# Hybrid decoder layer on one core: planner prices, slab release times, slack, and the sums of the last norm

## The chip, the cores and the metric

One core of one Trainium2 chip runs the whole layer in one launch. The metric is device time in microseconds (us). The kernel before was timed three times: 1110.89, 1110.3 and 1108.43 us, median 1110.3.

Engines are named as the profile names them: PE (TensorE matmuls), PEld (its weight loads), DVE (VectorE), ACT (ScalarE), POOL (GpSimd) and SP (SyncE, which issues all DMAs here).

## The reference, cut to what matters

One trunk layer on `x` of 1024 tokens by 1024 channels, float32, followed by a final RMSNorm:

```python
h = rmsnorm(x, norm_mix_w); proj = h @ w_in                # 3072 main columns + 8 gate logits
qkv = silu(causal_conv4(qkv)); q, k = l2norm(q), l2norm(k) # 4 heads of 128
o = gated_delta_rule_chunked(q, k, v, g, beta)             # per chunk: (I + A)^-1, then a scan of states
gdn_out = rmsnorm(o, gdn_norm_w) * silu(z)
lru_out = rg_lru(causal_conv4(lru_x) + b, ...) * gelu(lru_gate)   # 512 channels
x = x + concat(gdn_out, lru_out) @ w_out
u = relu(rmsnorm(x, norm_mlp_w) @ w_ff1)
x = x + (u * u) @ w_ff2
return rmsnorm(x, final_norm_w)
```

## The kernel before, in words

Channels lie on the 128 partitions and tokens along the free dimension; the 1024 tokens are two halves (`hf`) of 512. The common tile is a "slab" of 128x512 float32; there are 84 of them (`NS`). Each float32 product is made of three float32r matmuls (high x high, high x low, low x high).

The program has these stages: 24 column tiles of the input projection (matmuls into `pj`), between which the work of the four heads and of the LRU is placed; the output projection (`po`); the first feed-forward product (`pf`) and the second (`p`), both as a seven-product scheme for 2x2 blocks; and the last norm.

No engine's order is written by hand. The layer is first recorded as a list of operations, and `Plan.emit` then simulates the engines: `price` gives each operation a cost, `lag` the time until another engine sees its result, and the next operation is the one that can start first, with due times breaking near ties. The real instructions are issued in that order, so all of them carry line 376, where `emit` calls the engine. At run time each engine works through its own list in order and waits on semaphores where an operand or a buffer isn't ready. What the planner believes decides only the order and which buffer an operation gets.

Places that the change and the prediction touch:

- `price`, line 283: the cost of a POOL operation on n elements of a partition. `emit` adds a lag of 0.1 us between POOL operations that depend on each other.
- `admit`, line 298: a PE operation due between 30 and 1000 is held ready `SLACK` us later after an operand from another engine. The projections' own matmuls are due from 10000 on and have no such slack.
- `room` and lines 357 to 362: an operation that writes a new slab takes one that the plan has free by then, the latest one released. Line 382 notes when a slab is free again: 0.2 us after its last user's planned end.
- `invert32` and `rows32` (lines 768 to 808): POOL inverts the 32x32 diagonal blocks of a head, in 31 rounds of a product into `tm` and a subtraction from `V`. Round m reads the slab `N[m // 16]`. SP then moves the result into `Y`.
- `gd_k`, `gd_u`, `gd_q`, `gd_inv`, `gd_scan`: the heads' PE units between the projection's matmuls; `psK`, `psA`, `psP`, `psZ`, `pvs`, `psO` are their PSUM banks (eight banks in all). `gd_inv` begins with a DVE transpose of `Y` into a slab `YT`. `evac` empties a projection bank into `p` on DVE.
- The end, lines 1465 to 1479: the last product is done in two halves of 256 tokens. For each of four row tiles, `plus` adds the bank to `u2` on DVE, `squares` squares it on ACT, and `normed` sums the squares over partitions with matmuls against `onesd` into `n3p`, one pair of columns for each part; then come the root, `n3b`, and the scaled output `ot`.

Of the kernel before, what the change touches and what calls it, by code (L numbers as in the profile page):

```python
# [32 lines left out]
LOOK = 4  # L33
AHEAD = 100
TAIL = 4
SLACK = 1.3
LAND = 2.0
LATE = 2.5
SMALL = ("bv", "tr")
# [29 lines left out]
def lag(a, b):  # L69
    return LAG[a, b] if (a, b) in LAG else LAG_FROM[a] + (0.12 if b == "pe" else 0.0)  # L70
# [114 lines left out]
class Plan:  # L185
# [77 lines left out]
    @staticmethod  # L263
    def price(e, method, args, kw):
        out = kw.get("out", args[0] if args else None)
        src = [v for k, v in kw.items() if isinstance(v, View) and k in ("in_", "in0", "in1", "data0")]
        shape = out.shape if isinstance(out, View) else src[0].shape
        n = 1
        for d in shape[1:]:
            n *= d  # L270
        if e == "sy":
            return n * shape[0] * 4 / 300e3
        psum = any(v.root.tag == "m" for v in src)
        ptr = sum(isinstance(kw.get(k), View) for k in ("scalar", "scalar1", "scale", "bias"))
        if e == "ve":
            if method == "reciprocal":
                return 0.06 + 0.0066 * n
            return 0.067 + n * (0.00104 if method in TWO or psum else 0.00052) + 0.06 * ptr
        if e == "ac":
            return 0.0008333 * n + (0.051 if psum else 0.094) + 0.093 * ptr + (0.093 if "accum_out" in kw else 0.0)  # L280
        if method == "memset":
            return 0.036 + 0.00083 * n
        return 0.2 + 0.0021 * n

    def emit(self, engines, caps):
        ops = self.ops
# [6 lines left out]
        slots = {t: [(0.0, k) for k in range(n)] for t, n in caps.items()}  # L293
        table, dma = None, 0.0

        def admit(o):
            for e in o.engines:
                late = SLACK if e == "pe" and o.due < 1000.0 and o.due > 30.0 else 0.0
                ready[e].append((max([d.end + lag(d.eng, e) + (late if d.eng != "pe" else 0.0) for d in o.deps], default=0.0), o))

        def loads(o):

            return o.table is not None and o.table != table and not (o.table == "any" and table in WITH_TANH)
# [13 lines left out]
        def choose(strict):  # L317
            pick = None
            for e, lst in ready.items():
                if not lst:  # L320
                    continue
                look = []
                for t, o in (sorted(lst, key=lambda x: (x[1].due, x[1].seq))[:10] if e == "sy" else lst):
                    rt = room(o, strict)
                    if rt is None:
                        continue
                    s = max(t, free[e], rt)
                    if len(o.engines) > 1 and any(max(free[x], t) + o.cost[x] < s + o.cost[e] for x in o.engines if x != e):
                        continue
                    look.append((s, o))  # L330
                if not look:
                    continue
                first = min(s + HOLD * loads(o) for s, o in look)
                best = None
                for s, o in look:
                    if s + HOLD * loads(o) > first + WAIT[e]:
                        continue
                    key = o.due + SWITCH * loads(o)
                    if best is None or (key, o.seq) < best[0]:
                        best = (key, o.seq), s, o  # L340
                if pick is None or best[1] < pick[1]:
                    pick = e, best[1], best[2]
            return pick
# [4 lines left out]
        for _ in range(len(ops)):  # L348
            pick = choose(True) or choose(False)
            if pick is None:  # L350
                left = [o for o in ops if o.eng is None and not o.wait]
                raise RuntimeError("no room: " + ", ".join(f"{o.engines}.{o.calls[0][0]}:{[r.nm for r in o.roots if r.real is None]}" for o in left[:30])
                                   + str({t: len(s) for t, s in slots.items()}))
            e, s, o = pick
            for x in o.engines:
                ready[x] = [q for q in ready[x] if q[1] is not o]
            for r in o.roots:
                if r.real is None:
                    sl = slots[r.tag]
                    r.slot = max((x for x in sl if x[0] <= s), default=min(sl))  # L360
                    sl.remove(r.slot)
                    r.real = r.make(r.slot[1])
            c = o.cost[e]
            if e == "sy":
                small = any(r.tag in SMALL for r in o.roots)
                free[e] = s + (0.62 if small else 0.45)
                dma = max(dma, free[e] + 0.65) + c
                o.end = dma + (LATE if small else LAND)
            else:
                if loads(o):  # L370
                    table = "exp" if o.table == "any" else o.table
                    c += LOAD
                free[e] = o.end = s + c
            o.eng = e
            for method, args, kw in o.calls:
                getattr(engines[e], method)(*[v.ap() if isinstance(v, View) else v for v in args],  # L376
                                            **{k: v.ap() if isinstance(v, View) else v for k, v in kw.items()})
            for r in o.roots:
                r.users -= 1
                r.end = max(r.end, o.end)  # L380
                if not r.users:
                    slots[r.tag].append((r.end + 0.2, r.slot[1]))
            for q in o.next:
                q.wait -= 1
                if not q.wait:
                    admit(q)
# [4 lines left out]
def layer(ctx: ExitStack, tc: tile.TileContext, xT, win, wba, prm, cst, wga, wgx, wout, w1, w2, out):  # L391
# [4 lines left out]
    pe, ve, ac, gp, sy = (pl.engine(n) for n in engines)  # L396
# [9 lines left out]
    def slab(nm, dt=F32):  # L406
        return pl.tile(sp, [P, 512], dt, "s", nm)

    def pair(nm, dt=F32):
        return [slab(nm + "0", dt), slab(nm + "1", dt)]  # L410

    def bank(nm):
        return pl.tile(mpool, [P, 512], F32, "m", nm)
# [31 lines left out]
    def mm3(ps, w, x, first, last, order=((0, 0), (0, 1), (1, 0))):  # L445
        n = 0
        for a, b in order:
            pe.matmul(ps, lhsT=w[a], rhs=x[b], start=first and n == 0, stop=last and n == 2)
            n += 1
# [91 lines left out]
    def when(i):  # L541

        return 14.0 * i
# [448 lines left out]
    def chain(t):  # L992
        return pl.at(due=t)
# [9 lines left out]
    with pl.at(due=-2000.0):  # L1003
        for hf in range(2):
            hs = slice(hf * 512, hf * 512 + 512)
            ps0 = [bank(f"g0_{i}") for i in range(2)]
            ss = slab("ss1")
            for k in range(KT):
                pl.due = -2000.0 + 10 * k + 100 * hf
                if hf == 0:  # L1010
                    xraw[0, k] = slab("xraw")
                    sy.dma_start(out=xraw[0, k], in_=xT[k * P:(k + 1) * P, hs])
                    if k in (0, 2, 4):
                        n = 4 if k == 4 else 2
# [101 lines left out]
    ss = pair("ss2")  # L1116
# [31 lines left out]
    for n, d in enumerate(DO):  # L1148
        i = len(MT) + n
        t = when(i)  # L1150
        split(i + 1)
        for hf in range(2):
# [6 lines left out]
            with chain(t + 7 + 7 * hf):  # L1159
# [3 lines left out]
                x = bm[d, hf] = slab("bm")  # L1163
# [21 lines left out]
    def tf(g):  # L1185
        return t0 + g * 19.1
# [32 lines left out]
    for g in range(NG):  # L1219
        t = tf(g)  # L1220
        ps, y = {}, {}
# [60 lines left out]
    def ts(st, g):  # L1282
        return begin[st] + g * 2.72 * len(STAGES[st])
# [50 lines left out]
    def wsl(g, i, d):  # L1334
        return tuple(t[:, d * P:(d + 1) * P] for t in W2[g, i])
# [7 lines left out]
    def plus(x, y):  # L1343
        ve.tensor_tensor(out=x, in0=y, in1=x, op=ALU.add)
# [40 lines left out]
    def squares(x, n=512):  # L1385
        y = slab("sq3")[:, 0:n]
        ac.activation(out=y, in_=x, func=AF.Square)
        return y
# [6 lines left out]
    for st, prods in enumerate(STAGES):  # L1395
        tail = TAIL if st == 3 else 0
        pd = {}
        for g0 in range(0, NG, 2):
# [6 lines left out]
            for d in range(4):  # L1405
                for i in prods:
# [10 lines left out]
                    with chain(ts(st, g0) - 100):  # L1417
                        if i in (1, 7, 5):
                            x = {1: p1, 7: u3, 5: p5}[i][d] = slab(f"p{i}_")
# [10 lines left out]
            for x, k, g in residual[st]:  # L1430
                if g in gs:
                    with chain(ts(st, g) + 3):
                        plus(x[k[0] % 4], load_x2(*k, st, g))
                        if x is p5:
                            y = squares(p5[k[0] % 4])
                            if k[0] == 4:
                                ss = y
                            else:
                                plus(ss, y)
        t = begin[st] + 87  # L1440
# [7 lines left out]
        if st == 2:  # L1448
            with chain(t - 40):
                s1 = None  # L1450
                for x in [p1[d] for d in range(4)] + [u3[d] for d in range(4)]:
                    y = squares(x)
# [6 lines left out]
    t = ts(3, NG - TAIL)  # L1459
# [5 lines left out]
    for o in (0, 256):  # L1465
        qs = slice(o, o + 256)
        parts = []
        for d in range(4):
            ps = bank("p2")[:, 0:256]
            for g in range(NG - TAIL, NG):  # L1470
                with pl.at(due=10000.0 + t + o / 50 + 0.1 * d), pl.unit(PIECE / 2):
                    mm3(ps, wsl(g, 3, d), tuple(x[:, qs] for x in UU[g, 3]), g == NG - TAIL, g == NG - 1)
            with chain(t - 100):
                x = u2[d][:, qs]
                plus(x, ps)
                parts.append((squares(x, 256), t))
        parts.insert(1, (ss[:, qs], t))
        X = [u2[d][:, qs] for d in range(4)] + [p5[d][:, qs] for d in range(4)]
        normed(X, parts, 512 + o, 256, t + o / 50, [4, 5, 6, 7, 0, 1, 2, 3], True)

# [64 lines left out]
```

## Time and profile before

| | |
|---|---|
| runs | 1108.43 to 1110.89 us, median 1110.3 |
| profiled execution, its own time | 1107.9 us |
| its span, first to last instruction | 1105.8 us |
| mean granted PE clock | 0.993 |
| PE busy | 1087.3 us (98%), 5399 matmuls |
| DVE busy | 864.8 us (78%) |
| ACT busy | 552.1 us (50%) |
| POOL busy | 100.5 us (9%), 282 instructions |

Times of the trace are counted from the span's start. A row of a stretch in order of time has start, duration, engine, line, operation, output and inputs with their shapes, the count where several were merged, and in brackets the idle time of the engine ahead of it with what ended it. Busy PE time includes matmuls that run at a lower clock, and ends of matmuls are modelled. Who ended a wait is inferred from semaphores.

### The profile page before, as it was taken

How to read it: one execution, taken by the hardware profiler on the slowest of the kernel's cores; microseconds unless marked ns; L12 is line 12 of the kernel's file. 1: busy time of each engine (PE TensorE's matmuls, PEld its weight loads, DVE VectorE, ACT ScalarE, POOL GpSimd, SP SyncE). 2: the span in 40 equal slices, each digit the busy share in tenths (PEclk: the TensorE clock that was granted, in tenths of full speed). 3: DMA queues.
4: the chain of work that ended last, by engine and by line, in shares of the span. 5: the costliest groups of instructions: out<-in, count | busy, mean ns of one | idle time of the engine just before them, and what ended most of it. 6: DMA issues, size and time to landing. Idle time of an engine off the chain costs nothing. (4 is left out here: it accounts for less than half of the span.)

```text
span 1105.8 us, 15998 instructions
## 1 busy us (share of the span) xinstructions
PE 1087.3 (98%) x5399; PEld 895.7 (81%) x5399; DVE 864.8 (78%) x1672; ACT 552.1 (50%) x1134; POOL 100.5 (9%) x282
## 2 busy tenths in 40 slices
PE   9999989999999999999999999999999999999996
PEld 7788867888787878888888888888888888888886
DVE  7878665797779776598988888887965767865796
ACT  8559634545485955453333333333444544564442
POOL 0004857026000000000000000000000000000000
PEclk9999989999999999999999999999999999999998
DMA  7133513233212144424544444434856565677382
GB/s 239 39 96 86 125 27 103 68 89 97 78 58 58 39 152 133 153 95 147 197 146 158 146 160 143 171 140 174 283 179 220 180 206 184 206 237 241 125 296 84
DMA packets 124225, 159.17 MB, mean 144 GB/s; under 512 B 56392, under 2 KB 59120, under 8 KB 124144
## 3 DMA queue, kind: packets, MB, share of 16 engines
q1 hardware_dynamic: 124144, 158.16, 44.3%
q8 instruction: 42, 0.69, 0.3%
q14 instruction: 39, 0.32, 0.1%
HBM read 115.11 MB, written 43.01 MB: 143 GB/s over the span
## 5 line engine op out<-in xcount | busy, mean ns | idle before, releaser
L376 PE MATMUL pj<-xh,w 128*128 128x512 f32 x704 | 244.9, 406 | 0.5 <-DVE p L376 0.5
L376 PEld LDWEIGHTS pj<-xh,w 128*128 128x128 f32 x704 | 133.1, 189 | 28.6 <-DVE p L376 1.1
L376 PE MATMUL pj<-xl,w 128*128 128x512 f32 x352 | 138.2, 393 | 0.0
L376 ACT ACTIVATE c<-c 128x512 f32<-128x512 f32 x64 | 40.4, 632 | 85.6 <-DVE c L376 80.7
L376 PE MATMUL po<-mxh,w 128*128 128x512 f32 x256 | 79.3, 390 | 0.8 <-ACT mxh L376 0.8
L376 ACT CAST w<-r 128x512 fp32r<-128x512 f32 (+1 forms) x62 | 51.3, 828 | 54.7 <-PE pf L376 37.8
L376 DVE SCALAR_TENSOR_TENSOR y<-p,pr,y 128x512 f32<-128x512 f32 (+3 forms) x96 | 71.5, 750 | 6.5 <-ACT y L376 4.1
L376 PEld LDWEIGHTS pj<-xl,w 128*128 128x128 f32 x352 | 66.9, 190 | 10.5
L376 DVE TENSOR_TENSOR w<-r,w 128x512 fp32r<-128x512 f32 (+1 forms) x62 | 58.7, 947 | 19.2 <-ACT w L376 18.8
L376 POOL TENSOR_TENSOR tm<-V,N 128x60 f32<-128x60 f32 (+24 forms) x124 | 48.4, 390 | 128.6 <-DMA N<-bn 69.3
L376 PEld LDWEIGHTS po<-mxh,w 128*128 128x128 f32 x256 | 48.0, 188 | 11.1 <-ACT mxh L376 1.2
L376 PE MATMUL po<-mxl,w 128*128 128x512 f32 x128 | 49.9, 390 | 0.7 <-DVE mxl L376 0.7
L376 POOL TENSOR_TENSOR V<-V,tm 128x60 f32<-128x60 f32 (+24 forms) x124 | 45.3, 365 | 9.7
L376 DVE SCALAR_TENSOR_TENSOR c<-c,n2B 128x512 f32<-128x512 f32 x64 | 43.8, 689 | 1.2
L376 PE MATMUL pf<-B5h,w 128*128 128x512 f32 x128 | 42.7, 394 | 0.0
L376 PE MATMUL pf<-B6h,w 128*128 128x512 f32 x128 | 42.3, 390 | 0.0
L376 ACT ACT_TABLE_LOAD x27 | 34.6, 1283 | 3.5 <-DVE y L376 2.4
L376 DVE TENSOR_TENSOR c<-pf,u 128x512 f32<-128x512 f32 x48 | 32.8, 686 | 0.5
L376 ACT CAST v6h<-s 128x512 fp32r<-128x512 f32 x16 | 10.0, 622 | 41.0 <-DVE s L376 41.0
L376 PEld LDWEIGHTS pf<-B5h,w 128*128 128x128 f32 x128 | 24.0, 188 | 6.9 <-DVE c L376 2.0
L376 PE MATMUL p<-u3h,v3h 128*128 128x512 f32 (+1 forms) x80 | 28.4, 355 | 0.7 <-DVE u L376 0.7
L376 PEld LDWEIGHTS po<-mxl,w 128*128 128x128 f32 x128 | 24.0, 188 | 6.0 <-DVE mxl L376 1.0
(512 smaller groups left out, 2976.2 us busy)
## 6 DMA issues: line engine op xcount, KB each, us to landing
w2r<-w SPq DMA_DIRECT2D x112, 256.0 KB, 3.5
ur<-ud SPq DMA_DIRECT2D x112, 256.0 KB, 4.9
r<-w SPq DMA_DIRECT2D x32, 512.0 KB, 3.7
ud<-c SPq DMA_DIRECT2D x64, 256.0 KB, 2.1
ud<-ut SPq DMA_DIRECT2D x48, 256.0 KB, 2.1
r<-win SPq DMA_DIRECT2D x22, 512.0 KB, 4.0
xraw<-xT SPq DMA_DIRECT2D x16, 256.0 KB, 5.2
r<-wout SPq DMA_DIRECT2D x8, 512.0 KB, 4.5
```

Of the source, the lines that this page charges most:

```text
L376: getattr(engines[e], method)(*[v.ap() if isinstance(v, View) else v for v in args], **{k: v.ap() if isinstance(v, View) else v for k, v i ...
```

## The change

A POOL operation is priced at 0.22 + 0.0023 n in place of 0.2 + 0.0021 n. `SLACK` is 1.0 in place of 1.3. A slab or a DRAM tile whose last planned user runs on POOL (`gp`) or is a DMA of SP (`sy`) counts as free 2.0 us after that user's end, where it was 0.2; all others stay at 0.2. In the end stage, the squares of row tiles 0 to 2 and the earlier sum `ss` are added up on DVE into one tile, and `normed` gets two parts (that sum and the squares of tile 3) in place of five.

```diff
-SLACK = 1.3
+SLACK = 1.0
...
-        return 0.2 + 0.0021 * n
+        return 0.22 + 0.0023 * n
...
-                    slots[r.tag].append((r.end + 0.2, r.slot[1]))
+                    slots[r.tag].append((r.end + (2.0 if e in ("gp", "sy") else 0.2), r.slot[1]))
...
                 x = u2[d][:, qs]
                 plus(x, ps)
-                parts.append((squares(x, 256), t))
-        parts.insert(1, (ss[:, qs], t))
+                y = squares(x, 256)
+                if d == 0:
+                    plus(y, ss[:, qs])
+                    parts.append((y, t))
+                elif d < 3:
+                    plus(parts[0][0], y)
+                else:
+                    parts.append((y, t))
         X = [u2[d][:, qs] for d in range(4)] + [p5[d][:, qs] for d in range(4)]
```

## Rows read from the trace of the kernel before

**Rows 1.** The page's first part: busy time, share and instructions of each engine.
```profile
PE 1087.3 (98%) x5399; PEld 895.7 (81%) x5399; DVE 864.8 (78%) x1672; ACT 552.1 (50%) x1134; POOL 100.5 (9%) x282
```

**Rows 2.** PE's waits, 100 to 400 us: us in total, times, longest.
```profile
PE psA L376 <- DVE p L376: 3.8, 1, 3.8
PE po L376 <- ACT mxh L376: 0.8, 1, 0.8
PE psP L376 <- DVE S L376: 0.7, 1, 0.7
PE po L376 <- DVE mxl L376: 0.7, 1, 0.7
PE pj L376 <- DVE p L376: 0.5, 1, 0.5
PE psr L376 <- DVE p L376: 0.3, 1, 0.3
```

**Rows 3.** Stretches: from:to, length, busy PE PEld DVE ACT POOL, clock, DMA share, GB/s.
```profile
131.00:138.90 7.90, 7.90 (x55) 6.44 (x55) 4.29 (x6) 4.18 (x15) 6.65 (x17) 1.00 0.47 125
138.90:142.94 4.04, 0.28 (x3) 0.04 (x1) 1.04 (x3) 0.02 (x1) 3.26 (x11) 0.73 0.00 0
142.94:151.07 8.13, 8.13 (x65) 5.95 (x66) 4.97 (x15) 4.73 (x20) 6.64 (x20) 0.51 0.01 3
```

**Rows 4.** PE in order of time, 122 to 152 us.
```profile
138.58 0.60 PE L376 MATMUL psK<-cs,y 128*128 128x128 f32 x4
142.94 2.08 PE L376 MATMUL psA<-y 128*128 128x128 f32 x8 [3.77 <-DVE p L376]
```

**Rows 5.** DVE in order of time, 122 to 152 us.
```profile
122.49 1.23 DVE L376 TENSOR_TENSOR w<-r,w 128x1024 fp32r<-128x1024 f32 x1 [0.23 <-ACT w L376]
...
135.76 1.61 DVE L376 SCALAR_TENSOR_TENSOR y<-p,pr,y 128x512 f32<-128x512 f32 x2
141.87 0.45 DVE L376 STREAM_TRANSPOSE YT<-Y 128x256 f32<-128x256 f32 x1 [4.49 <-POOL tm L376]
142.24 0.65 DVE L376 TENSOR_TENSOR p<-pj,n1B 128x512 f32<-128x512 f32 x1
```

**Rows 6.** POOL in order of time, 90 to 152 us.
```profile
96.16 0.47 POOL L376 TENSOR_TENSOR tm<-V,N 128x31 f32<-128x31 f32 x1 [69.32 <-DMA N<-bn]
...
122.34 0.27 POOL L376 TENSOR_TENSOR V<-V,tm 128x42 f32<-128x42 f32 x1
122.69 1.15 POOL L376 TENSOR_TENSOR tm<-V,N 128x35 f32<-128x35 f32 x1
...
126.39 0.21 POOL L376 TENSOR_TENSOR V<-V,tm 128x8 f32<-128x8 f32 x1
...
128.33 0.24 POOL L376 TENSOR_TENSOR tm<-V,N 128x31 f32<-128x31 f32 x1
...
141.53 0.30 POOL L376 TENSOR_TENSOR tm<-V,N 128x64 f32<-128x64 f32 x1
```

**Rows 7.** PE's weight loads: their waits, 485 to 1078 us.
```profile
PEld pf L376 <- DVE c L376: 2.0, 11, 0.2
```

**Rows 8.** DVE in order of time, 217 to 224 us.
```profile
221.85 0.35 DVE L376 SCALAR_TENSOR_TENSOR S<-S,egl,pvs 128x128 f32<-128x128 f32 x1
```

**Rows 9.** PE in order of time, 217 to 224 us.
```profile
222.25 0.49 PE L376 MATMUL pvs<-S,y 128*128 128x128 f32 x2
```

**Rows 10.** The matmuls of `n3p` grouped: duration ns min/median/max, first and last start.
```profile
L376 PE MATMUL n3p<-onesd,sq x48: 164/250/271, 1052.1 to 1097.3; 128*128 128x1 f32 x48
```

**Rows 11.** PE in order of time, 1084 us to the end.
```profile
1088.10 2.29 PE L376 MATMUL n3p<-onesd,sq 128*128 128x1 f32 x20
1090.25 0.36 PE L376 MATMUL p<-u3h,v3h 128*128 128x256 f32 x1
...
1095.66 0.28 PE L376 MATMUL p<-u3h,v3l 128*128 128x256 f32 x1
1096.90 0.61 PE L376 MATMUL n3p<-onesd,sq 128*128 128x1 f32 x4 [0.97 <-ACT sq L376]
```

**Rows 12.** DVE in order of time, 1084 us to the end.
```profile
1090.20 0.38 DVE L376 TENSOR_SCALAR ms<-n3p 128x1 f32<-128x1 f32 x2 [1.48 <-PE n3p L376]
...
1093.30 0.42 DVE L376 TENSOR_TENSOR ot<-n3b,p__9670 128x256 f32<-128x256 f32 x1 [0.73 <-PE n3b L376]
...
1095.98 0.42 DVE L376 TENSOR_TENSOR u<-p,u 128x256 f32<-128x256 f32 x1
```

## The prediction

> **What bounds the kernel now.** I read the engines' totals first, then PE's waits, then stretches around the longest of them, then the last 25 us. PE is busy for 1087.3 of the 1105.8 us span [rows 1]; DVE comes next with 864.8. A change can thus gain in two ways: less PE work, or less PE time lost inside or beside that 98%. The list of PE's waits between 100 and 400 us is headed by one wait of 3.8 us, a `psA` product held by DVE's `p`; the other five are under 0.9 us [rows 2]. The busy figure hides a second loss: in the stretch of 8.13 us after that wait PE counts as fully busy, but the granted clock is 0.51, so the matmuls run at 1.2 instead of 2.4 GHz; before the wait it was 1.00 [rows 3].
>
> Who holds PE? PE finished `psK` at 138.58 + 0.60 = 139.18 and started `psA` at 142.94 [rows 4]. On DVE, `y` ended at 137.37, then DVE stood idle for 4.49 us until 141.87, when the transpose into `YT` could start; `p`, which empties the bank that `psA` needs, is queued behind that transpose [rows 5]. What released it was POOL's `tm`. The POOL step that ended at 141.83 is the one of 128x64 [rows 6]: with w = 31 - m and r = m // 4 + 1 that is m = 15, the last step that reads the slab `N[0]` of the second head. So `YT` was given the slab of `N[0]`, and the written order believed POOL to be past it.
>
> **The POOL price and the slab times.** The planner's clock can be compared with the trace. A head's 62 steps hold 2 x 1560 elements a partition; with the lag of 0.1 between dependent POOL steps the old price makes 62 x 0.3 + 0.0021 x 3120 = 25.2 us, the new one 62 x 0.32 + 0.0023 x 3120 = 27.0. The first head took from 96.16 to 126.60, 30.4 us [rows 6]. In the second head, the 31 steps to the last reader of `N[0]` hold 1656 elements: 12.8 us by the old price, 13.7 by the new, 13.5 measured (128.33 to 141.83). So the old plan had the slab free 5.2 + 0.7 = 5.9 us too early, less the 0.2 it adds; DVE waited 4.49, so the plan had left about 1.2 us to spare. The new plan is 3.4 - 0.2 = 3.2 us early in POOL's time, and the added 2.0 takes that to 1.2, as much as was spare. If the same slab is chosen again the wait is about nothing; if the slab is not yet free in the new plan, the choice (the latest one that is free) falls on another.
>
> What goes with it: 4.04 - 0.28 = 3.76 us of PE idle, and 8.13 x (1 - 0.51) = 3.98 us at the lower clock [rows 3], together 7.7. What is late next? Without the wait, DVE would do `YT` (0.45) and `p` (0.65) from 137.37 and be done near 138.5, before PE's 139.18, so `psA` follows `psK` at once. I leave 0.2 us for a rest: **-7.5 us**. Bounds: 0 (a like wait elsewhere) to -7.7.
>
> The trace speaks against one price for all steps: the first two heads run the same 62 shapes, and POOL steps near in size take 0.27 us or 1.15. The 1.15 one, from 122.69, lies over a DVE subtraction with two SBUF inputs that runs from 122.49 to 123.72 [rows 5, 6]. So POOL's lateness follows DVE's order, which the change redraws; that is the first rival below. The Trainium skill says this in "SBUF — State Buffer", section "SBUF: two separate sides": DVE (in an instruction with two SBUF inputs) and a GpSimd instruction lock a shared pair of ports against each other, for a whole instruction. The trace agrees: that POOL step ends at 123.84, 0.12 us after DVE's. By the rule POOL's delay can come back anywhere in the new order, and the sum is then that of the first rival.
>
> The later release also holds for slabs whose last user is a load or store: the `ud` stores of the first feed-forward product, seven for each of 16 groups, and the turned tiles of the heads. It adds no instruction, and nothing to SP's queue. In the feed-forward stage the only named wait of PE is 11 weight loads of at most 0.2 us [rows 7]: the next group's operands are there ahead, and that lead hides a planned delay of 1.8 us. I cost it at 0; without that cover it is at most 16 x 1.8 = 29 us. Up to POOL's first step at 96.16 nothing on the path changes its price, so the order there should be much the same.
>
> **SLACK 1.3 to 1.0.** A PE unit of the heads and of the LRU is believed ready 0.3 us sooner after a DVE or ACT operand. It holds for units due between 30 and 1000. By the code a head has 10 units in `gd_inv` and 23 in `gd_scan`; with `gd_q` (4) of three heads, `gd_k` and `gd_u` (4) of the last, whose due times alone pass 30, and 16 LRU products that is 132 + 12 + 4 + 16 = 164. Matmuls wait in order, so a unit that comes too early holds the projection behind it. Most have room: of 76 hand-offs to `pvs` that I matched, 8 come within 0.5 us of their operand; at the closest `S` ended at 222.20 and `pvs` began at 222.25 [rows 8, 9]. A tenth of 164, each losing 0 to 0.3 us, is 0 to 4.9 us. Below nothing: shorter chains could end PE's small waits, the two of `po` with 1.5 us above all [rows 2]. I take **+1.5**, nearer to the close pair's few than to all.
>
> **The last norm.** Before, each half has five parts, each with two columns; a column takes two matmul records: 40 of the 48 `n3p` records [rows 10] (8 are of the earlier half of the output). The new code has two parts: 16 records, 24 fewer. Twenty ran from 1088.10 to 1090.25, 0.1075 each [rows 11]: 2.6 us of PE. PE works with no gap from there to its last product at 1095.66, all on the path: DVE took `u` at 1095.98, as soon as that product ended, and the rest is a fixed chain of square, sum, root and scaling. What is added are six DVE additions of 128x256 at 0.42 us (by the row of `u`) = 2.5 us. DVE has idle of 1.48 and 0.73 us there [rows 12], and the additions for parts 0 to 2 are due before the last product ends. If that cover is gone, three of them stand in front of the last `u`: 3 x 0.42 = 1.3. So -2.6 to -1.3; I take **-2.2**, DVE having been on time.
>
> **Sum.** -7.5 + 1.5 - 2.2 = -8.2 us against the profiled execution (span 1105.8, its own time 1107.9, so 2.1 us around it). That execution is 2.4 us under the median of 1110.3 and just under the lowest of the three. I put the difference on the median: 1110.3 - 8.2 = 1102.1, so **1102 us**.
>
> **Rivals.**
> 1. The long wait moves. Again a DVE step stands behind POOL or a transfer that is late by 3 to 4 us, PE waits, the clock falls: 7.7 us come back. For it: POOL's uneven steps, and an order redrawn from about 90 us on. Against: there was one such wait in the whole trace, and the slabs concerned now have 2 us more. Time: 1110.3 + 1.5 - 2.2 = 1109.6, no measurable change.
> 2. The smaller slack decides: PE meets its operands late all along the heads. A third of the 164 units losing 0.3 us is 16.4 us: 1110.3 - 7.5 - 2.2 + 16.4 = 1117, slower. It makes the kernel slower from 12 us, that is 40 units. For it: 8 of 76 are already close, and one full clock loss (4 us) would stand for 13 units. Against: the lead of most is well over 0.5 us.
> 3. The plan does not do what it says: another slab with the same fault is taken and the tail's additions stand in the way: 1110.3 + 1.5 - 1.3 = 1110.5. It counts with rival 1.
> 4. The redrawn order also loses the small waits (0.8, 0.7, 0.7, 0.5 and 0.3 us in [rows 2]) and the slack costs nothing: 1110.3 - 7.7 - 2.6 - 3.0 = 1097.
>
> **How the numbers follow.** Forecast 0.48, its own range 1099 to 1105; rival 1 with 3: 0.20; rival 2: 0.20; rival 4: 0.12. About 0.2%, 2.2 us, is what a measurement of this kernel can tell from no change. Faster by that: forecast and rival 4 (0.60), and a little of rival 1, where a shorter wait comes back: 0.62. Within it: the rest of rival 1, 0.17. Slower: rival 2 and a bad rival 1, 0.21. The range runs from rival 4 at 1097 to 1113, past rival 1 and into the milder cases of rival 2; about a tenth is left out on each side.
>
> **What would show it.** Right: no PE wait over 2 us between 100 and 400 us; a granted clock of 1.00 in all slices until the last PE work; no DVE step released by a POOL `tm`; 24 `n3p` matmuls in the trace, and from the end of the last 128x256 product to the end of the span about 10 us as before. Wrong: a new PE wait of over 3 us with a low clock behind it (rival 1), a dozen or more new PE waits on `S`, `vs` or `vh` (rival 2), PE waits in the feed-forward stage (the cover of the stored slabs), or a gap between the last product and `u` (the tail). The prediction fails if the time stays within 1108 to 1112 although the wait at 139 us is gone.

## The result: 1098.7 us, and the profile after

The changed kernel took 1098.72 us (median of four, 1098.05 to 1099.57); the kernel before, beside it, 1110.06. The ratio is 0.99, 95% interval 0.9883 to 0.9917: 11.3 us less. On another chip it took 1099.13 us against 1111.18, ratio 0.989 (0.9873 to 0.9907). The forecast was 1102, range 1097 to 1113.

The profiled execution took 1098.3 us, its span is 1096.2; of before 1107.9 and 1105.8. So the two traces account for 9.6 us, and 1.7 of the medians' difference are not in them (the tail, below). The page's first line, which answers [rows 1]:

```profile
PE 1079.7 (98%) x5375; PEld 890.0 (81%) x5375; DVE 866.2 (79%) x1678; ACT 555.7 (51%) x1137; POOL 102.8 (9%) x282
```

24 matmuls fewer, six DVE steps more, and 7.6 us less PE time, part of it by the clock. PE's waits between 100 and 400 us, as in [rows 2] (total, times, longest):

```profile
PE po L376 <- DVE mxl L376: 1.2, 1, 1.2
PE psQ L376 <- DVE U L376: 0.8, 1, 0.8
PE pvs L376 <- DVE vs L376: 0.7, 1, 0.7
PE psT L376 <- issue: 0.2, 1, 0.2
```

The 3.8 us of `psA` is gone; 2.9 us are left of 6.8. The stretches that answer [rows 3], of the changed kernel:

```profile
131.00:141.57 10.57, 10.57 (x76) 8.74 (x75) 7.36 (x12) 7.08 (x28) 8.96 (x21) 1.00 0.26 70
141.57:151.07 9.50, 9.32 (x98) 7.10 (x99) 8.87 (x33) 4.54 (x20) 7.78 (x23) 1.00 0.05 9
```

The clock is 1.00 in both, where it was 0.51 for 8.13 us. The steps themselves, to hold against [rows 4, 5]: DVE, then PE in order of time.

```profile
136.84 1.61 DVE L376 SCALAR_TENSOR_TENSOR y<-p,pr,y 128x512 f32<-128x512 f32 x2
138.37 0.68 DVE L376 TENSOR_TENSOR p<-pj,n1B 128x512 f32<-128x512 f32 x1
...
139.71 0.45 DVE L376 STREAM_TRANSPOSE YT<-Y 128x256 f32<-128x256 f32 x1
```
```profile
140.08 0.60 PE L376 MATMUL psK<-cs,y 128*128 128x128 f32 x4
140.51 1.06 PE L376 MATMUL psA<-y 128*128 128x128 f32 x8
```

`YT` no longer waits for POOL, though POOL's 128x64 `tm`, the releaser of before, now ends at 143.29, later than its 141.83 in [rows 6]: `YT` was given another slab. `p` stands ahead of it, and `psA` follows `psK` at once.

The tail, to hold against [rows 10 to 12]: the matmuls of `n3p` grouped, then PE, then DVE in order of time.

```profile
L376 PE MATMUL n3p<-onesd,sq x24: 164/250/250, 1043.4 to 1086.2; 128*128 128x1 f32 x24
```
```profile
1084.36 0.28 PE L376 MATMUL p<-u3h,v3l 128*128 128x256 f32 x1
1084.48 0.50 PE L376 MATMUL n3p<-onesd,sq 128*128 128x1 f32 x4
1085.42 0.71 PE L376 MATMUL n3b<-cs,n3r 128*128 128x128 f32 x4 [0.44 <-DVE n3r L376]
1085.96 0.50 PE L376 MATMUL n3p<-onesd,sq 128*128 128x1 f32 x4
1088.76 1.19 PE L376 MATMUL n3b<-cs,n3r 128*128 128x128 f32 x4 [2.29 <-DVE n3r L376]
```
```profile
1084.68 0.42 DVE L376 TENSOR_TENSOR u<-p,u 128x256 f32<-128x256 f32 x1 [0.33 <-PE p L376]
...
1086.17 0.42 DVE L376 TENSOR_TENSOR ot<-n3b,p__9670 128x256 f32<-128x256 f32 x1 [0.80 <-PE n3b L376]
...
1087.60 0.15 DVE L376 TENSOR_TENSOR rst<-n3r 128x2 f32<-128x2 f32 x1
...
1088.46 0.15 DVE L376 SCALAR_TENSOR_TENSOR n3r<-rst,n3r 128x2 f32<-128x2 f32 x1
```

The last product starts at 1084.36, 11.3 us sooner than before, but the end comes only 9.6 sooner. The first half's `n3b` (1085.42) and its scaled outputs now lie behind the last product: DVE runs its eight `ot` steps between the small steps of the second half's root, and `n3b` of that half waits 2.29 us.

Where the 9.6 us came from, by the starts of the same instructions in the two traces:

| mark | before | after | sooner by |
|---|---|---|---|
| first `psA` | 77.6 | 77.9 | -0.3 |
| first scan product `pvs` | 163.3 | 156.2 | 7.1 |
| last `po` | 475.1 | 467.2 | 8.0 |
| first 128x256 product | 1079.3 | 1071.6 | 7.8 |
| last 128x256 product | 1095.7 | 1084.4 | 11.3 |
| end | 1105.8 | 1096.2 | 9.6 |

### The profile page after: what moved, and what is told of

The parts are those of the page before. It is cut to its first block, busy times and chain, and to the rows that moved or that the text cites. A ratio compares the mean times of both kernels' runs of the same rounds, so it can differ in the third digit from the quotient of the medians.

```text
span 1096.2 us, 15972 instructions
## 1 busy us (share of the span) xinstructions
PE 1079.7 (98%) x5375; PEld 890.0 (81%) x5375; DVE 866.2 (79%) x1678; ACT 555.7 (51%) x1137; POOL 102.8 (9%) x282
## 5 line engine op out<-in xcount | busy, mean ns | idle before, releaser
L376 POOL TENSOR_TENSOR V<-V,tm 128x60 f32<-128x60 f32 (+24 forms) x124 | 48.7, 393 | 9.7
```

## The experiments

Theory A, the prediction's: three parts that add up, price and release worth 7.5 us, the smaller slack a small loss, the sums 2.2 us. Against it stood the rivals of the prediction, above all that the long wait moves. The first four kernels hold parts of the change against the kernel before, all on one chip (before: 1111.29 us).

**Price and release alone.**

```diff
-        return 0.2 + 0.0021 * n
+        return 0.22 + 0.0023 * n
...
-                    slots[r.tag].append((r.end + 0.2, r.slot[1]))
+                    slots[r.tag].append((r.end + (2.0 if e in ("gp", "sy") else 0.2), r.slot[1]))
```

> Only the POOL price and the 2.0 us release of slabs used last by POOL or SP; SLACK 1.3 and the five-part norm as before. Theory A (the wait of the YT transpose on the slab of N[0], with the low clock behind it, is what the change removes): 7.5 to 8 us off, about 1102 us, no PE wait over 2 us between 100 and 400 us, granted clock 1.00 until the last PE work. Rival B (the smaller slack redraws the order and so removes the wait): little, 1109 to 1111, the wait still there. Rival C (the norm's sums bring most): 1110.

Measured: 1112.85 us, ratio 1.0025 (1.001 to 1.0041). No gain; theory A falls here. The wait at 139 us is gone, as A said, and the first `pvs` comes 5.0 us sooner; but all of it is given back around 220 us. PE's projection matmuls alone (`pj`) in two stretches of this kernel (columns as in [rows 3] without ACT and POOL), then all its work in two more:

```profile
204.00:215.40 11.40, 6.74 (x24) 3.79 (x23) 0.28 (x1) 1.00 0.10 18
215.40:229.10 13.70, 0.04 (x2) 0.01 (x1) 0.69 (x1) 0.67 0.08 22
```
```profile
215.40:220.00 4.60, 2.33 (x29) 1.82 (x28) 3.72 (x9) 1.91 (x5) 0.00 (x0) 1.00 0.08 11
220.00:233.70 13.70, 12.04 (x70) 9.96 (x71) 10.66 (x40) 3.50 (x17) 0.00 (x0) 0.50 0.15 39
```

For 13.7 us there is practically no projection matmul, the work that fills the time between dependent steps of the heads. PE is busy for 2.33 us of the first 4.60, and then the clock is 0.50 for 13.7 us. Rival 1 of the prediction happens: the lost time moves, though not to a step behind POOL. No single long wait marks it: between 100 and 400 us PE's longest one in this kernel is 1.2 us.

**The squares alone.**

```diff
-                parts.append((squares(x, 256), t))
-        parts.insert(1, (ss[:, qs], t))
+                y = squares(x, 256)
+                if d == 0:
+                    plus(y, ss[:, qs])
+                    parts.append((y, t))
+                elif d < 3:
+                    plus(parts[0][0], y)
+                else:
+                    parts.append((y, t))
```

> Only the squares of the last norm summed on DVE. Theory A: the wait at 139 us stays as it is, and the end gains 1.9 us by the stretch from the first 128x256 product to the end of the span (26.5 us before, 24.6 after): 1108.2 us. Rival C: 3.5 us or more (the last product comes 3.5 us sooner in the changed kernel), 1106.5 or lower. If the additions stand in the way of DVE: 0 to -1.

Measured: 1106.24 us, ratio 0.9962 (0.9948 to 0.9975): 4.2 us less by the ratio, 5.0 by the medians, more than the 2.2 of the sum. In its trace the stretch from the first 128x256 product to the end is 24.4 us, 2.1 less than before. The other 2 to 3 us do not show there; the last experiment takes that up.

**The slack alone.**

```diff
-SLACK = 1.3
+SLACK = 1.0
```

> Only SLACK 1.3 to 1.0. Theory A: the heads' PE units before 139 us are due too early to have slack, so the wait on N[0]'s slab stays unless a moved slab breaks it; from the first pvs to the last po the change gained 0.8 us, so 1108 to 1111 us. Rival B: 1102 us and no wait. My own prediction's term was +1.5 us: 1111.6.

Measured: 1110.31 us, ratio 0.9996 (0.9982 to 1.0009): by itself the smaller slack costs nothing and gives nothing. PE's long wait is still there:

```profile
PE psA L376 <- DVE p L376: 4.3, 1, 4.3
```

**All but the slack** (price, release and squares, `SLACK` 1.3; the change with that one line undone).

> The changed kernel with SLACK put back to 1.3. Theory A: price, slabs and norm bring nearly all: 1099 to 1101 us, 0 to 2 us above the changed kernel. Rival B: 1107 to 1109, the wait is back. By my prediction's term for the slack it would be 1.5 us under the changed kernel, 1097.2.

Measured: 1108.09 us, ratio 0.9976 (0.9963 to 0.9989). The time is rival B's, but what its trace shows is again the stretch near 220 us. All work of this kernel in three stretches, then its `pj` alone in the same:

```profile
206.00:217.40 11.40, 11.37 (x76) 9.95 (x74) 6.95 (x25) 5.32 (x28) 0.00 (x0) 1.00 0.10 18
217.40:230.40 13.00, 8.46 (x87) 6.87 (x87) 10.88 (x34) 4.54 (x16) 0.00 (x0) 0.78 0.09 23
230.40:236.00 5.60, 5.60 (x33) 4.54 (x35) 4.04 (x19) 1.39 (x9) 0.00 (x0) 0.59 0.48 114
```
```profile
206.00:217.40 11.40, 6.72 (x24) 3.77 (x22) 0.22 (x1) 1.00 0.10 18
217.40:230.40 13.00, 0.03 (x1) 0.03 (x1) 0.69 (x1) 0.78 0.09 23
```

What ended this stretch without projection matmuls is told by PE's next `pj`, and what held that up by DVE in order of time:

```profile
206.91 1.06 PE L376 MATMUL psA<-y 128*128 128x128 f32 x8
...
208.46 1.06 PE L376 MATMUL psA<-y 128*128 128x128 f32 x8
...
230.37 0.79 PE L376 MATMUL pj<-xh,w 128*128 128x512 f32 x1 [0.54 <-DVE U L376]
```
```profile
226.32 0.35 DVE L376 TENSOR_SCALAR vh<-pvs,cj 128x128 f32<-128x128 f32 x1
227.19 0.16 DVE L376 TENSOR_TENSOR cj<-rk,beta 128x8 f32<-128x8 f32 x1
...
228.01 1.64 DVE L376 SCALAR_TENSOR_TENSOR U<-psA,cj,DT 128x128 f32<-128x128 f32 x6
```

The projection waits for a bank that `U` empties: the fourth head's `psA`, made at 206.91. `U` needs that head's `cj`, and `cj` is a small tile with three buffers (line 686), so the fourth head's is the first head's, which is read until the last `vh` of that head's scan. Here that `vh` begins at 226.32 and `cj` follows at 227.19. So the new theory A2: the fourth head's `psA` holds PSUM banks until the first head's scan is over; when the open projection column is used up sooner, no bank is left for the next, and PE runs dry. With slack 1.0 the scan is shorter: from the first `pvs` to the fourth head's `cj` it is 61.6 us in the changed kernel, 66.9 here and 67.6 with price and release alone (63.9 before). The length of the scan alone does not make the gap, though: in the kernel with the later `N` slabs (below) it is 66.6 us, and no stretch without `pj` is longer than 3.2 us. What goes with the gap in the traces is when the fourth head's second `psA` (tokens 512 to 1023) takes its bank. In the three kernels that have the gap (price and release, this one, and price alone) it starts 1.6 to 2.5 us after the first, so that both banks are held for about 20 us; in every other kernel with three buffers it starts 8.5 to 12.8 us after it. In the changed kernel the first starts at 197.61 and the second here:

```profile
207.86 1.06 PE L376 MATMUL psA<-y 128*128 128x128 f32 x8
```

The changed kernel's `pj` from 211 us on, to hold against the 13 us above:

```profile
211.00:224.00 13.00, 7.29 (x27) 4.22 (x26) 0.00 (x0) 1.00 0.05 9
```

**Four buffers, without the smaller slack**: the test of A2.

```diff
-cj=small("cj", [P, NC], 3), egl=small("egl", [P, NC], 3), pn=small("pn", [P, NC], 3),
-sk=small("sk", [P, NC], 3))
+cj=small("cj", [P, NC], 4), egl=small("egl", [P, NC], 4), pn=small("pn", [P, NC], 4),
+sk=small("sk", [P, NC], 4))
```

> Price, slabs and norm changed, SLACK 1.3 (the kernel of the run that kept the old slack), and four buffers instead of three for cj, egl, pn and sk. Theory A2: there the fourth head's U waits for the first head's cj buffer, holds two PSUM banks from psA to U (23 us), and the projection has no bank: 13 us without a pj matmul, 3.4 us of PE waits and 10.2 us of low clock. With a fourth buffer U comes 10 us or more sooner, no pj gap over 6 us, no low clock near 225 us: 1098 to 1101 us. Rival: the banks are held by the interleaved scans, not by U: 1106 to 1109, the gap stays.

Measured: 1101.59 us, ratio 0.9925 (0.9912 to 0.9937). By the ratios that is 5.7 us under the kernel without the buffers, which ran on another chip; it is 0.6 us above A2's range and far from the rival's. `cj` and `pj` of this kernel:

```profile
211.44 0.17 DVE L376 TENSOR_TENSOR cj<-rk,beta 128x8 f32<-128x8 f32 x1
```
```profile
213.35:226.00 12.65, 7.67 (x30) 4.89 (x29) 0.68 (x1) 1.00 0.39 116
```

`cj` no longer waits for the scan, 30 projection matmuls run where there was one, the clock stays at 1.00: A2 holds, although the two `psA` stand as close together as before (204.65 and 206.20). All four small tiles got a fourth buffer; that `cj` is the one that mattered is read from the rows.

**Four buffers on the changed kernel.**

> The changed kernel with four buffers for cj, egl, pn and sk. Theory A2: the bank shortage near 220 us is mild there (pj gap 4.0 us, one wait of 0.8 us), so 0 to 1.5 us off: 1097 to 1099. Rival (every redraw of the order is a lottery of one long wait, about 8 us): 1105 or more in one case of two.

Measured: 1097.08 us (1096.5 to 1100.26), ratio 0.9881 (0.9866 to 0.9897). Since the changed kernel had been timed on another chip, both ran again on one:

> The changed kernel again, as the measure for the next kernel on the same chip. Both theories: 1098 to 1099 us, about 11 under the kernel before, no PE wait over 2 us and no stretch of more than 5 us without a projection matmul between 100 and 400 us.

> The changed kernel with four buffers instead of three for a head's small tiles cj, egl, pn and sk. Theory (the fourth head's psA banks are held until the first head's scan gives its buffers back): even in the changed order the banks are held from 197.6 to 222.5 us, with four buffers the hold was 14 us, so the median comes out 1 to 2 us under the changed kernel's on the same chip, near 1097. Rival (the changed order has room for that hold, its projection matmuls fill the time): no difference beyond 0.5 us.

Measured: 1099.13 us, ratio 0.989 (0.9873 to 0.9907), against 1098.39, ratio 0.9881 (0.9866 to 0.9897). The intervals overlap nearly whole: the rival stands, with slack 1.0 the buffers give nothing that can be told from zero. The last `pvs` does come 8.9 us sooner in that trace (345.7 for 354.6), but the last `po` at 467.3 against 467.4: the heads end earlier, the projection, which has to be done anyway, does not. The two kernels with four buffers tell something else about the slack: 0.9925 with 1.3 (0.9912 to 0.9937) and 0.9881 with 1.0 (0.9866 to 0.9897) lie clear of each other. So the smaller slack still brings 4.9 us by the ratios where there is no gap left to undo.

**Only the slabs `N[0]`, `N[1]` later**, everything else as before: is the slab that `YT` takes the cause of the wait at 139 us?

```diff
-                    slots[r.tag].append((r.end + 0.2, r.slot[1]))
+                    slots[r.tag].append((r.end + (8.0 if r.nm in ("N0", "N1") else 0.2), r.slot[1]))
```

> The kernel before, but the slabs N0 and N1 alone count as free 8 us after their last POOL step (all others 0.2 us; POOL price, slack and norm as before). Theory A1: the wait of 3.8 us near 139 us comes from the YT transpose being given N[0]'s slab, so it is gone here, 7.5 us, unless the order that follows starves PE of projection matmuls elsewhere: 1102 to 1103 if not, 1108 to 1112 with a stretch of over 10 us without a pj matmul near 220 us. Rival: the wait comes from DVE's or ACT's own lateness, then it stays at 139 us, 1110.

Measured: 1107.57 us, ratio 0.9976 (0.9964 to 0.9989), between the two ranges that were expected. `YT` waits for nothing and the first `pvs` comes 6.0 us sooner (7.6 counted from the first `psA`), so the cause is the slab. But only 3.2 us of it (4.8) reach the last `po`: waits of 1.3, 1.3 and 1.2 us stand elsewhere in the heads, and there is no gap near 220 us.

**Only the POOL price.**

```diff
-        return 0.2 + 0.0021 * n
+        return 0.22 + 0.0023 * n
```

> The kernel before with only the dearer POOL price (0.22 + 0.0023 n), slabs free 0.2 us after their user as before, slack 1.3. Theory A (the price alone is enough to give YT another slab or a later place): no PE wait on DVE's p near 139 us, first scan product pvs 5 to 7 us earlier than 163.3. Rival B (by the price alone the plan is still 3.2 us early in POOL's time with 1.2 to spare, so the release of 2.0 us is what is needed): a wait of about 2 us near 139 us remains, the first pvs 0 to 3 us earlier. In both the time is within 1106 to 1113, since the gain of 139 us can be given back near 220 us.

One execution, 1109.67 us, too few for a ratio. PE's longest waits between 100 and 400 us:

```profile
PE po L376 <- DVE mxl L376: 1.7, 1, 1.7
PE psZ L376 <- DVE at L376: 1.4, 1, 1.4
PE pj L376 <- ACT w L376: 1.1, 1, 1.1
```

The wait on `p` is gone by the price alone, so theory A is right in this, and the 2.0 us of release are not needed for it. The first `pvs` comes 3.6 us sooner rather than 5 to 7 (new waits of 1.0 and 0.4 us on `Y` and `p`), and it too has 8.7 us without `pj` near 220 us with a clock of 0.51 behind them.

**First-half outputs on POOL**: the eight `ot` steps that stand among the second half's root, half of them moved from DVE to POOL in the changed kernel.

```diff
-                    if end and d >= 4:
+                    if end and d >= 4 and a == 512:
+                        if j == 0:
+                            rb = slab("rb")[:, 0:n]
+                            ac.copy(out=rb, in_=pb[:, 0:n])
+                        gp.tensor_tensor(out=y, in0=rb, in1=X[d], op=ALU.mult)
+                    elif end and d >= 4:
```

> The changed kernel; in the end, for the first 256 tokens, the four products into ot of row tiles 4 to 7 run on POOL from a copy of n3b that ACT makes. In the changed kernel DVE runs without a pause from 1086.2 us to the last ot, 16 ot in all, which is why the last stretch (last product to the end) grew by 1.7 us. If DVE sets the end: four ot of 0.33 us less, 1.3 us off, 1097.4. If the fixed chain of the second half sets it: 0.

Measured: 1100.47 us, ratio 0.9914 (0.9899 to 0.9929), no gain. POOL and then DVE in order of time:

```profile
1089.90 0.73 POOL L376 TENSOR_TENSOR ot<-rb,p__9729 128x256 f32<-128x256 f32 x1
1090.59 0.72 POOL L376 TENSOR_TENSOR ot<-rb,p__9759 128x256 f32<-128x256 f32 x1
```
```profile
1089.72 0.24 DVE L376 TENSOR_TENSOR rst<-n3r 128x2 f32<-128x2 f32 x1
...
1090.28 0.37 DVE L376 SCALAR_TENSOR_TENSOR rst<-rst,ms 128x2 f32<-128x2 f32 x1
1090.68 0.65 DVE L376 SCALAR_TENSOR_TENSOR n3r<-rst,n3r 128x2 f32<-128x2 f32 x1
```

The same small DVE steps took 0.15 us in the changed kernel. Each ends just as a POOL step ends: 1090.65 against 1090.63, 1091.33 against 1091.31. `n3b` waits 3.60 us instead of 2.29, and from the end of the last product to that of the span it is 13.3 us instead of 11.6. The Trainium skill, "SBUF — State Buffer", section "SBUF: two separate sides", says that a DVE instruction with two SBUF inputs and a GpSimd instruction exclude each other for a whole instruction; these rows agree, and show the direction in which DVE is the one that waits.

**The saved matmuls put back.** The squares-only kernel with three more products of the first sum in each half, into a bank that nothing reads: 24 one-column records, the DVE sums unchanged.

```diff
+        if end:
+            dead = bank("n3p")
+            for k in range(3):
+                with chain(parts[0][1]):
+                    with pl.unit(0.12 * m):
+                        for c in range(m):
+                            pe.matmul(dead[:, c:c + 1], lhsT=parts[0][0][:, c * P:(c + 1) * P], rhs=onesd, start=True, stop=True)
```

> The kernel before with only the squares of the last norm summed on DVE, and the 24 one-column matmul records that this saves put back: in each half the first sum is multiplied three more times into a bank that nothing reads. The DVE additions are as in the squares-only kernel, which took 1106.2 against 1111.3. Theory A (the gain of the squares is the one-column matmuls: their PE time, and a fall of the granted clock after them that most executions of the kernel before show by their mean clock, .987 to .990 against .993): 1109 to 1111, mean clocks again below .990 in most runs. Rival B (the gain is the DVE sums' place in the order alone, the matmuls only cost PE time): 1106.2 + 2.6 x 0 to 1, 1106 to 1108.8, mean clocks at .991 and above.

Measured: 1110.82 us, ratio 0.9994 (0.9983 to 1.0005), where the squares alone had 0.9962 (0.9948 to 0.9975). The whole gain is gone, so it comes from the matmuls and not from where the DVE sums stand. All work of the tail: this kernel, then the squares-only kernel, each from its first 128x256 product.

```profile
1080.21:1094.60 14.39, 14.23 (x119) 14.04 (x119) 12.52 (x31) 6.17 (x14) 0.00 (x0) 1.00 0.01 2
1094.60:1098.72 4.12, 4.12 (x19) 3.83 (x19) 1.18 (x3) 0.00 (x0) 0.00 (x0) 0.50 0.15 50
```
```profile
1080.80:1093.84 13.04, 12.89 (x107) 12.69 (x107) 12.19 (x29) 6.17 (x14) 0.00 (x0) 1.00 0.01 2
```

With the matmuls back the clock falls to 0.50 while PE has products left: 4.12 us of them cost half of that, 2.1 us. Ahead of the fall PE was at work, a run of 20 one-column matmuls at 1091.14 among it. The kernel with the later `N` slabs, which has the old tail, shows the same in its trace: 0.50 from 1087.90 to 1094.70, PE busy throughout, after 20 such matmuls at 1084.88. In the profiled execution of before the clock fell only at 1099.9, behind the last product. But of 65 executions of before that ran beside these kernels, 43 have a mean clock under 0.9905 and a median of 1111.7 us, the other 22 have 1108.6; ten of the eleven with the matmuls put back are under 0.9905, and none of the twelve with the squares alone is. A mean clock does not say where the fall was; that it is the tail's in all of these is taken from the traces that have it. The other fall that comes and goes, 3.4 us near 33 us (last section), does not explain them by itself: it takes 3.4 x 0.5 / 1105.8 = 0.0015 from 0.993, which leaves 0.991. The fourteen traces agree on the tail. Of the six with 48 `n3p` matmuls four have a fall ahead of the last product, and from the first to the last 128x256 product they take 17.9 to 19.4 us; the other two (before, and the slack alone) take 16.3. None of the eight with 24 has it, and all of them take 12.8.

## Why the prediction was right, and where its steps were not

**Price and release, -7.5.** The first `pvs` comes 7.1 us sooner, 7.4 counted from the first `psA`: wait and low clock both went, and the cause is shown by the `N` slabs alone (7.6 by the same count). But not all of it belongs to price and release. With slack 1.3 the two bring 5.2 us: from the first `psA` to the first `pvs` it is 85.7 us before, 80.5 with price and release alone, 80.6 with all but the slack, and 78.3 in the changed kernel. The other 2.2 came with the smaller slack. Two more corrections. "If the same slab is chosen again the wait is about nothing": another slab was chosen. And the two edits are not both needed; the price alone, or a later release of two slabs alone, removes the wait.

**The slack, +1.5.** This is the step that failed, in sign and in kind. From the first `pvs` to the last `po` the changed kernel gained another 0.8 us. I costed the slack as a delay of single units, each on its own. What the runs show instead: by itself it does nothing (0.9996); without it the other three parts give 0.9976 instead of 0.99 and 0.989, so it is worth 8 to 10 us in this combination. One part of that is the gap near 220 us, which four buffers remove as well (5.7 us). Another part is there without the gap (4.9 us with four buffers), about 2 of it ahead of the first `pvs`. By the marks the gap goes with a second `psA` of the fourth head close behind the first, rather than with a long scan; no run tests that alone. The terms do not add: price and release +2.8 us alone, squares -4.2, slack -0.4 (ratios times 1111.3) make -1.8; together they are -11 to -12. That my sum of separate terms came close is luck: rival 1 really happens in the order with the old slack, and the new slack, which I had booked as a loss, happens to undo it.

**Rival 1** had a chance of 0.20 and was the nearest: in three of the four kernels that have the new price but the old slack the lost time only moves (price alone by one execution; the fourth kernel is the one with four buffers). Its mechanism was mis-told: not a step behind POOL or a transfer, but a bank held by a product whose consumer waits for a small tile of another head. Its sign, a new PE wait of over 3 us, would have missed it: the longest in those three is 1.7 us, and it shows as a stretch without `pj` with a low clock behind it. **Rival 2**, a time lost on many hand-offs, did not occur: PE's waits in the heads' stage became fewer.

**The last norm, -2.2.** The traces have 1.85 for that stretch. "The rest is a fixed chain" failed: the products end 3.6 us earlier, since 24 one-column matmuls are gone and the first half's `n3b` and four `n3p` of the second half moved behind them, but the stretch from the start of the last product to the end grew from 10.2 to 11.9 us, since by the rows DVE now scales the first half's outputs there (moving half of them to POOL did not test this, as POOL's steps then held DVE's). Over all executions the term is larger, the squares alone gave 4 to 5 us, since the clock's fall in the tail went with the matmuls.

**The step from trace to median.** I took the 2.4 us between the profiled execution and the median of before as staying. It did not: after, the same difference is 0.4 us. The clock's fall in the tail, absent from the profiled execution and, by the mean clocks, present in most others, went with the matmuls. So of the 3.4 us by which 1102 was too high, 1.4 are in the traces (9.6 where the sum was 8.2, the slack's term above all) and 2.0 in this step.

Not settled: why the clock falls behind the run of one-column matmuls in some executions and not in others; how the smaller slack shortens the first head's scan by 5 us and moves the second `psA`, which was read from the marks and not tested on its own; and where the 4.9 us that it brings with four buffers come from, beyond the 2 ahead of the first `pvs`.

## What to carry to other kernels

In a kernel whose order comes from a planner, edits of its beliefs need not add, as they did not here: a new order can have its own worst place. So time them together and alone, and look for where the gain was given back before dropping an edit. A matmul result that waits for its consumer holds a PSUM bank, and a small tile with one buffer too few in another loop can be what holds it. Compare the profiled execution's time and mean clock with those of the other runs: a loss that most runs have can be missing from the one trace that was read.

## What the runs showed of the hardware that I had not expected

In the kernel with the later `N` slabs the granted clock fell to 0.50 for 6.8 us (1087.90 to 1094.70) with PE counted as fully busy throughout and for the 6.9 us ahead of it. Near 33 us it fell to 0.50 for 3.4 us in the profiles of seven of the kernels, where the first `pj` came 1.6 to 2.4 us later than in before's; of the two profiles of the changed kernel with four buffers, one has this fall and the other does not. POOL and DVE delay each other both ways: a POOL step of 35 columns took 1.15 us under a DVE step [rows 5, 6], and a DVE step of two columns took 0.65 us behind POOL's where it took 0.15 without.
